# A decoder layer on one core: up-projection units 2 to 9 with the weights stationary, and one chain of the down-projection kept in PSUM over all groups

## The chip, the cores and the metric

The kernel runs on one core of a Trainium2 chip. The metric is the device time of one execution, in microseconds; three timed executions of the kernel before have a median of 1039.24 us (1039.18 to 1039.37). The profile is one more execution, recorded by the hardware profiler. Five engines work side by side and each takes its own instructions in order: PE (matrix products; PEld is its loading of the stationary operand), DVE and ACT (elementwise work, and the only two here that read PSUM), POOL and SP (here mostly queues that issue transfers).

## The reference, cut to what matters

The layer mixes a gated convolution, a pooling and an attention, adds the result to x, and then runs a feed-forward block. The change is in the feed-forward block alone:

```python
D_MODEL, SEQ = 2048, 256
D_FF = ((8 * D_MODEL // 3 + 255) // 256) * 256            # 5632
...
h = rmsnorm(x, g_ffn[l])
u = causal_dwconv(h @ w_up[l], ffn_conv_w[l]) + ffn_conv_b[l]   # 2 * D_FF columns, 3 taps over positions
gate, val = jnp.split(u, 2, axis=-1)
x = x + (jax.nn.silu(gate) * val) @ w_down[l]
return rmsnorm(x, g_final)
```

Everything is float32.

## The kernel before, in words

**Products.** A float32 product is made of three products of a narrower type. A weight tile that has landed in a `raw` buffer is split: ACT copies it to `hi` (rounded), DVE subtracts to get `lo`, the rest (`split_piece`, lines 131 and 132; for the down-projection's blocks `Blocks.split`, lines 254 and 255). The activations are held split as well. A product is high x hi, high x lo and low x hi. One tile of weights holds 128 x 2048 numbers, 1 MB. There are three `hi` buffers and three `lo` buffers, so that tile i can be split only when PE is done with tile i-3. Tiles are numbered in the order of `stream`; `next_tile` keeps loads three tiles and splits two tiles ahead of use.

**Units and groups.** The 5632 hidden columns are 11 units of 512. A unit has a gate part (w = 0) and a value part (w = 1), each 512 columns of `w_up`, and takes 8 tiles, called t0 to t7 below: four for the gate, four for the value. Units go in pairs as five groups (group 0 is units 0 and 1, and so on); unit 10 stands alone. Units 0 and 1 share a scheme of their own (`up_mixed`) that the change doesn't touch.

**`up` (lines 967 to 1006).** The activations are stationary (128 x 128) and the weights move, 512 columns at a time: a tile holds 4 blocks of 128 of the inner dimension, and is used by 2 blocks of tokens x 4 x 3 = 24 products of 512 columns. Results `pu` have tokens on the partitions, and after four tiles ACT scales them by each token's norm factor into `z` (line 1005). `up_finish` (lines 1071 to 1108) then turns `z` by 8 products with the identity (`pz`, line 1079) so that channels lie on the partitions, and works on each of the 4 blocks of channels: ACT applies the third tap and the bias (line 1087), DVE adds the other two taps (line 1089), ACT applies silu to gates (line 1093), and DVE multiplies value by gate into `u_raw`, a part of the buffer `ffn` (line 1103). The turning waits in the list `todo` and is run in the middle of the next tile.

**Down-projection.** When a group is done, `turn` builds eight combinations of its hidden values (`make_forms`, lines 881 to 899: seven DVE steps of 512 and one of 2048 elements, and ACT copies). While PE goes through the next group's units, `prod` is run 14 times between its tiles: seven products for each half of the output columns (p = 0 and 1), each of 12 matrix products on one tile of combined weights. The weights are combined by additions on DVE (`Blocks.add`, line 247) and by transfers that add (`Blocks.add_far`, line 244, on the POOL queue), issued from the splits of the products 0, 1 and 3. The seven products form three chains of sums in PSUM, `a`, `b` and `c`; a chain goes on adding in its bank, and after each product DVE adds the bank to the output rows `xt` (line 927). Chain `c` has one product, the sixth. The last group's p = 1 is done without combinations (`Plain`).

**Order.** `sched` gives the order by hand: no product in the first three tiles of a group, one after each of the next twelve, two after the last. So in the first unit of a group PE does t0, t1, t2, t3, product 0, t4, product 1, t5, product 2, t6, product 3, t7, product 4. The framework's scheduler then fixes the order of each engine's queue; it may pull single instructions of a later tile ahead where it takes them to be ready.

Of the kernel before, what the change touches and what calls it, by code (L numbers as in the profile page):

```python
# [9 lines left out]
F32 = mybir.dt.float32  # L10
F32R = mybir.dt.float32r
AF = mybir.ActivationFunctionType
# [3 lines left out]
P = 128  # L16
EPS = 1e-6
HPAD = 6
# [6 lines left out]
def kernel(  # L25
# [25 lines left out]
    def bank(name):  # L51
        return psum.tile([P, 512], F32, tag="bank", name=name)
# [42 lines left out]
    def cvec(name, i):  # L95
        c = col[name] + i
        return cols[:, c : c + 1]


    def src_a(w, k0, nk, c0, ncol):  # L100
        return w[k0 * P : (k0 + nk) * P, c0 : c0 + ncol].rearrange("(k p) c -> p k c", p=P)
# [52 lines left out]
    def next_tile():  # L154
        i = state["use"]
        state["use"] += 1
        advance(i + 1 + LOAD_AHEAD, i + 1 + SPLIT_AHEAD)
        return split.pop(i)
# [165 lines left out]
    def part_of(u, b):  # L324


        return (b // 2 % 2, b % 2 + b // 4 * 2) if u == 0 else (b // 4, b % 4)
# [50 lines left out]
                prods += [("plain" if isinstance(b, Plain) else "prod", b, i) for i in range(n)]  # L378
    for what, a, b in sched:
        if what == "up":  # L380
            w, q = part_of(a, b)
            plan_b(w_up, 4 * q, 4, w * D_UP + a * 512, 512, 4)
        elif what == "mixed" and isinstance(b, int):
            stream.append((up_blocks, None, b, 1))
        elif what == "mixed":
            plan_b(w_up, 4 * b[1], 4, (1 - b[0]) * D_UP + a * 512, 512, 4)
        else:
            stream.append((a, None, b, 1))
# [47 lines left out]
    def row_of(r, nm):  # L436

        pr = bank(f"prow_{nm}")
        row = cpool.tile([P, S], F32, name=f"row_{nm}")
        with tc.high_priority():  # L440
            for tb in range(TB):
                nc.tensor.transpose(
                    pr[:, tb * P : (tb + 1) * P], r[:, tb : tb + 1].to_broadcast([P, P]), ident
                )
            nc.scalar.activation(row, pr[:, :S], AF.Copy)
        return row
# [15 lines left out]
    def mm_a(ps, wt, actT, k0, nk, first, last):  # L462
        hi, lo = wt
        for kk in range(nk):
            k = k0 + kk
            cs = [slice(mi * P, (mi + 1) * P) for mi in range(len(ps))]
            for mi, c in enumerate(cs):
                nc.tensor.matmul(  # L468
                    ps[mi], hi[:, kk, c], actT[:, k, :], start=first and kk == 0, stop=False
                )  # L470
            for mi, c in enumerate(cs):
                nc.tensor.matmul(
                    ps[mi][:, S:], lo[:, kk, c], actT[:, k, :S],
                    start=False, stop=last and kk == nk - 1,
                )
# [123 lines left out]
    def split_into(o, src, n=S):  # L599

        nc.scalar.activation(o[:, :n], src, AF.Copy)
        nc.vector.tensor_tensor(o[:, n:], src, o[:, :n].bitcast(F32), op=ALU.subtract)
# [300 lines left out]
    def prod(bl, i):  # L903
        hi, lo = next_tile()

        chain, first, tb, right, op = (
            ("a", True, 0, 0, ALU.add),
            ("b", True, 1, 1, ALU.add),
            ("a", False, 0, 1, ALU.subtract),
            ("a", False, 1, 1, ALU.subtract),  # L910
            ("b", False, 0, 1, ALU.add),
            ("c", True, 0, 0, ALU.add),
            ("a", False, 1, 0, ALU.add),
        )[i]
        if first:
            chains[chain] = bank(f"pp_{bl.gi}_{bl.p}_{chain}")
        ps = chains[chain]
        for j in range(4):
            ah, al = bl.stationary(i, j)
            for n, (a, b) in enumerate(((ah, hi), (ah, lo), (al, hi))):  # L920
                nc.tensor.matmul(  # L921
                    ps, a, b[:, j, :], start=first and j == 0 and n == 0,
                    stop=j == 3 and n == 2, skip_group_check=True,
                )
        c0 = bl.p * 1024 + right * 512
        o = xt[:, tb, c0 : c0 + 512]
        nc.vector.tensor_tensor(o, o, ps, op=op)
# [34 lines left out]
    rawd = [ffn[:, 1 + i, :].rearrange("p (j c) -> p j c", c=512) for i in range(3)]  # L962

    u_last = h2T[:, : 4 * UNITS[-1], :]
    up_ps, up_gates, todo, r_2 = {}, {}, [], []

    def up(u, b):


        w, q = part_of(u, b)  # L970
        if q == 0:
            up_ps[w] = [bank(f"pu{u}_{w}_{tb}") for tb in range(TB)]
        ps = up_ps[w]
        hi, lo = next_tile()
        for tb in range(TB):
            for kk in range(4):
                k = 4 * q + kk
                ah = h2T[:, k, tb * P : (tb + 1) * P]
                al = h2T[:, k, S + tb * P : S + (tb + 1) * P]
                for n, (x_, y_) in enumerate(((ah, hi), (ah, lo), (al, hi))):  # L980
                    nc.tensor.matmul(  # L981
                        ps[tb], x_, y_[:, kk, :],
                        start=k == 0 and n == 0, stop=k == KC - 1 and n == 2,
                    )
            if tb == 0 and todo:
                todo.pop(0)()
        if u == 0 and b == 0:
            for k in range(8, 16, 2):
                split_turned(turn_pair(xt, k, "x2"), h2T, "g_ffn", k)
            r_2.append(rstd_sum(ssq4, "x2"))  # L990
        if u == 0 and b == 1:
            h2_8 = h2T[:, :8, :].bitcast(F32)
            nc.vector.tensor_tensor(u_raw, h2_8[:, :, :S], h2_8[:, :, S:], op=ALU.add)
            make_forms(
                u_raw, None, lambda half: sums[:, 1:5, half], (), "h2",
                up_blocks.buf("b12").rearrange("p j (f t) -> p j f t", t=P),
            )
            for name in ("b11", "b22", "b12"):
                up_blocks.load(name)
        if q < 3:  # L1000
            return
        z = []
        for tb in range(TB):
            z.append(spool.tile([P, 512], F32, tag="w2k", name=f"z_{u}_{w}_{tb}"))
            nc.scalar.activation(z[tb], ps[tb], AF.Copy, scale=r_2[0][:, tb : tb + 1])  # L1005
        todo.append(lambda: up_finish(u, w, z))

    def up_mixed(u, what):

# [61 lines left out]
    def up_finish(u, w, z):  # L1071

        pt = []
        for c in range(4):
            if c % 2 == 0:
                pt.append(bank(f"pz{u}_{w}_{c}"))
            for tb in range(TB):
                o = c % 2 * S + tb * P
                nc.tensor.transpose(pt[-1][:, o : o + P], z[tb][:, c * P : (c + 1) * P], ident)  # L1079
        outs = []  # L1080
        for c in range(4):
            v = pt[c // 2][:, c % 2 * S : (c % 2 + 1) * S]
            m = w * NF + u * 4 + c
            tag, n, bufs = ("w1k", S, 6) if w else ("hpad", PAD + S, HPAD)
            t = spool.tile([P, n], F32, tag=tag, name=f"t_{u}_{w}_{c}", bufs=bufs)[:, :S]
            cw = [cvec("ffn_conv_w", j * 2 * NF + m) for j in range(3)]
            nc.scalar.activation(t, v, AF.Identity, bias=cvec("ffn_conv_b", m), scale=cw[2])  # L1087
            for s in (1, 2):
                nc.vector.scalar_tensor_tensor(  # L1089
                    t[:, s:], v[:, : S - s], cw[2 - s], t[:, s:], op0=ALU.mult, op1=ALU.add  # L1090
                )
            if w == 0:
                nc.scalar.activation(t, t, AF.Silu)
            outs.append(t)
        if w == 0:
            up_gates[u] = outs
            return
        gates = up_gates.pop(u)
        gi = [g for g, (a, n) in enumerate(group_of) if a <= u][-1]
        for c in range(4):  # L1100
            if gi < len(group_of) - 1:
                o = u_raw[:, (u - group_of[gi][0]) * 4 + c, :]
                nc.vector.tensor_tensor(o, gates[c], outs[c], op=ALU.mult)
            else:
                nc.vector.tensor_tensor(gates[c], gates[c], outs[c], op=ALU.mult)
                split_into(u_last[:, c, :], gates[c])
        if gi < len(group_of) - 1 and u == group_of[gi][0] + group_of[gi][1] - 1:
            turn(gi)

    def turn(gi):  # L1110
        make_forms(
            u_raw, lambda at, half: sums[:, at, half], lambda half: sums[:, 1:5, half],
            (0, 5, 6, 7) if gi == len(group_of) - 2 else (0, 5, 6), gi,
        )
# [118 lines left out]
                finish(1, c0, c1, r)  # L1233

    for what, a, b in sched:
        {"up": up, "mixed": up_mixed, "prod": prod, "plain": plain}[what](a, b)
    down_last(len(group_of) - 1)


# [29 lines left out]
```

## Time and profile before

| | |
|---|---|
| time, median of 3 | 1039.24 us |
| the profiled execution, its own time | 1039.66 us |
| its span in the profile | 1037.9 us |
| PE busy | 1026.7 us, 99% of the span |
| DVE busy | 820.5 us, 79% |
| ACT busy | 601.8 us, 58% |
| moved between memory and chip | 224.97 MB, 217 GB/s |

The profile lists busy time per engine, then groups of equal instructions by line (count, busy time, mean duration, idle time ahead of them), and the chain of work that ended last, followed back from the end. Busy times of PE groups overlap each other, since its products are pipelined; what a product costs is read from the distance of starts in the timeline.

### The profile page before, as it was taken

The page shows a single profiled execution, that of the slowest core. Times are in us where ns is not written, and L with a number is a line of the kernel's source. Part 1 is how long each engine was busy: PE and PEld are TensorE (multiplying, and loading weights), DVE is VectorE, ACT ScalarE, POOL GpSimd, SP SyncE. Part 2 cuts the span into 40 slices and gives each one's busy share as a digit, 9 for nine tenths or more (in the row PEclk, how much of TensorE's full clock was granted, in tenths as well). Part 3 has the DMA queues.
Part 4 walks back from the last instruction along what each step waited for, and adds up shares of the span by engine and source line. Part 5 has one row for each costly group of instructions (what it writes and reads, how often), then busy time and mean ns, then how long its engine had stood idle before and what let it go on. Part 6 is the DMA issues. An engine that isn't in the chain of part 4 may idle for free.

```text
span 1037.9 us, 12624 instructions
## 1 busy us (share of the span) xinstructions
PE 1026.7 (99%) x4970; PEld 861.9 (83%) x4970; DVE 820.5 (79%) x866; ACT 601.8 (58%) x654; POOL 64.1 (6%) x97
## 2 busy tenths in 40 slices
PE   9999999999999999999999999999999999999996
PEld 7888888888888888888888888888888888888885
DVE  5677686777869688978779787797878978789776
ACT  5965454544556576655556556665566655665653
POOL 0023500000001000000000000000000000000000
PEclk9999999999999999999999999999999999999998
DMA  9765465557775687687966878668786697867832
GB/s 321 254 214 191 146 201 175 191 191 240 220 262 176 155 259 243 197 253 203 259 224 201 255 204 260 219 199 258 208 260 216 194 265 209 258 218 191 282 118 81
DMA packets 125157, 224.97 MB, mean 217 GB/s; under 512 B 3970, under 2 KB 36010, under 8 KB 124970
## 3 DMA queue, kind: packets, MB, share of 16 engines
q1 hardware_dynamic: 113450, 201.09, 57.2%
q0 software_dynamic: 11616, 23.07, 13.6%
q8 instruction: 39, 0.64, 0.2%
q14 instruction: 20, 0.16, 0.1%
q10 hardware_dynamic: 32, 0.01, 0.0%
HBM read 222.06 MB, written 2.10 MB: 216 GB/s over the span
## 4 chain that ended last, share of the span: by engine, by line
PE 98%; DMA 1%; DVE 0%; SPq 0%; DVEq 0%; issue 0%; ACT 0%
PE pu L981 42%; PE pp_a L921 9%; PE pp_b L921 5%; PE pp_c L921 2%; PE pa_cb L468 2%; PE pa_pv L468 2%; PE pa_cx L468 2%; PE pa_cc L468 2%; PE po L504 2%; PE pp L1127 2%; PE po L501 2%; PE po L507 2%; PE pz L1079 2%; PE pm_a L1024 2%; PE pa_q L468 1%; PE pk L558 1%
## 5 line engine op out<-in xcount | busy, mean ns | idle before, releaser
L981 PE MATMUL pu<-hi,h2T 128*128 128x512 f32 x1280 | 409.4, 391 | 0.0
L132 DVE TENSOR_TENSOR lo<-raw,hi 128x2048 fp32r<-128x2048 f32 (+3 forms) x148 | 314.7, 2128 | 70.9 <-ACT hi L131 69.9
L131 ACT ACTIVATE hi<-raw 128x2048 fp32r<-128x2048 f32 (+3 forms) x148 | 264.3, 1789 | 110.5 <-issue 34.7
L981 PEld LDWEIGHTS pu<-hi,h2T 128*128 128x128 f32 x1280 | 240.3, 188 | 49.4
L981 PE MATMUL pu<-lo,h2T 128*128 128x512 f32 x640 | 249.5, 390 | 0.0
L255 DVE TENSOR_TENSOR lo<-ffn,hi 128x2048 fp32r<-128x2048 f32 x70 | 160.3, 2290 | 72.0 <-ACT hi L254 72.0
L254 ACT ACTIVATE hi<-ffn 128x2048 fp32r<-128x2048 f32 x70 | 134.0, 1916 | 105.1 <-PE pu L981 75.0
L981 PEld LDWEIGHTS pu<-lo,h2T 128*128 128x128 f32 x640 | 120.2, 188 | 25.1 <-DVE lo L132 0.7
L921 PE MATMUL pp_a<-hi,sums 128*128 128x512 f32 x288 | 94.5, 389 | 0.0
L1089 DVE SCALAR_TENSOR_TENSOR t<-pz,cols,t 128x255 f32<-128x255 f32 (+1 forms) x176 | 79.6, 478 | 10.2 <-ACT t L1087 9.2
L1087 ACT ACTIVATE t<-pz,cols 128x256 f32<-128x256 f32 x88 | 46.9, 558 | 48.1 <-DVE t L1089 24.2
L921 PEld LDWEIGHTS pp_a<-hi,sums 128*128 128x128 f32 x288 | 54.1, 188 | 11.2
L244 POOL DMA_DIRECT2D ffn<-in_w_down_dram x18 | 23.1, 1284 | 575.8 <-DVE ffn L247 454.3
L921 PE MATMUL pp_a<-lo,sums 128*128 128x512 f32 x144 | 56.0, 389 | 0.0
L1005 ACT ACTIVATE z<-pu,r_x 128x512 f32<-128x512 f32 x40 | 27.4, 686 | 39.7 <-PE pu L981 39.6
L247 DVE TENSOR_TENSOR ffn<-ffn 128x2048 f32<-128x2048 f32 x20 | 45.7, 2287 | 3.4 <-DMA ffn<-in_w_up_dram 3.4
L921 PE MATMUL pp_b<-hi,sums 128*128 128x512 f32 x144 | 47.3, 389 | 0.0
L921 PEld LDWEIGHTS pp_a<-lo,sums 128*128 128x128 f32 x144 | 27.0, 188 | 5.6
L921 PEld LDWEIGHTS pp_b<-hi,sums 128*128 128x128 f32 x144 | 27.0, 188 | 5.6
L468 PE MATMUL pa_cb<-hT,hi 128*128 128x512 f32 x96 | 30.7, 400 | 0.0
L468 PE MATMUL pa_pv<-hT,hi 128*128 128x512 f32 x96 | 30.2, 396 | 0.0
L468 PE MATMUL pa_cc<-hT,hi 128*128 128x512 f32 x96 | 30.2, 395 | 0.0
(292 smaller groups left out, 1477.1 us busy)
## 6 DMA issues: line engine op xcount, KB each, us to landing
raw<-in_w_up_dram SPq DMA_DIRECT2D x84, 1024.0 KB, 7.5
ffn<-in_w_down_dram SPq DMA_DIRECT2D x40, 1024.0 KB, 6.1
raw<-in_w_in_dram SPq DMA_DIRECT2D x28, 1024.0 KB, 5.0
ffn<-in_w_down_dram POOLq DMA_DIRECT2D x18, 1024.0 KB, 10.3
raw<-in_w_out_dram SPq DMA_DIRECT2D x12, 1024.0 KB, 5.1
raw<-in_w_kv_dram SPq DMA_DIRECT2D x4, 1024.0 KB, 7.3
outp<-in_w_out_dram SPq DMA_DIRECT2D x4, 1024.0 KB, 7.5
ffn<-in_w_up_dram SPq DMA_DIRECT2D x4, 1024.0 KB, 5.5
```

The lines of the kernel that those rows point to most:

```text
L131: nc.scalar.activation(hi[:, s, :], raw[:, s, :], AF.Copy)
L132: nc.vector.tensor_tensor(lo[:, s, :], raw[:, s, :], hi[:, s, :].bitcast(F32), op=ALU.subtract)
L244: nc.gpsimd.dma_start(self.buf(to), self.source(what), accum_op=ALU.add)
L247: nc.vector.tensor_tensor(self.buf(to), self.buf(to), self.buf(what), op=ALU.add)
L254: nc.scalar.activation(hi, raw, AF.Copy)
L255: nc.vector.tensor_tensor(lo, raw, hi.bitcast(F32), op=ALU.subtract)
L468: nc.tensor.matmul(ps[mi], hi[:, kk, c], actT[:, k, :], start=first and kk == 0, stop=False)
L921: nc.tensor.matmul(ps, a, b[:, j, :], start=first and j == 0 and n == 0, stop=j == 3 and n == 2, skip_group_check=True,)
L981: nc.tensor.matmul(ps[tb], x_, y_[:, kk, :], start=k == 0 and n == 0, stop=k == KC - 1 and n == 2,)
L1005: nc.scalar.activation(z[tb], ps[tb], AF.Copy, scale=r_2[0][:, tb : tb + 1])
L1087: nc.scalar.activation(t, v, AF.Identity, bias=cvec("ffn_conv_b", m), scale=cw[2])
L1089: nc.vector.scalar_tensor_tensor(t[:, s:], v[:, : S - s], cw[2 - s], t[:, s:], op0=ALU.mult, op1=ALU.add)
```

## The change

Units 2 to 9 go through a new function `up_turned`. A tile now holds 8 blocks of the inner dimension and 256 columns, and the weights are stationary: `mm_a`, which the input projection already uses, takes for each of the 8 blocks and each of the 2 sets of 128 columns one product of 512 moving columns (both parts of the activations with `hi`) and one of 256 (`lo`). Results have channels on the partitions at once, so that the turning by the identity and `z` are gone; a pair of 128-channel blocks is finished after two tiles, so that a unit has four pairs instead of two parts of four blocks. The norm factor, which was a scale per partition, becomes a row (`row_of`, once) that DVE multiplies by. Chain `c` of each half of the output keeps its bank over all groups and is added to `xt` once, after the last group that uses combinations.

```diff
     for what, a, b in sched:
         if what == "up":
+            if 1 < a < n_units - 1:
+                stream.append(
+                    (src_a(w_up, b % 2 * 8, 8, b // 4 * D_UP + a * 512 + b // 2 % 2 * 256, 256), 8, 256, 1)
+                )
+                continue
...
+        done = True
+        if chain == "c" and bl.gi is not None:
+
+            chain = f"c{bl.p}"
+            first = chain not in chains
+            done = not any(type(b) is Blocks and b.p == bl.p and b.gi > bl.gi for b in blocks)
...
+        if not done:
+            return
         c0 = bl.p * 1024 + right * 512
...
+    def up_turned(u, b):
...
+        w, pair, h = b // 4, b // 2 % 2, b % 2
+        if h == 0:
+            up_ps[w] = [bank(f"pu{u}_{w}_{pair}_{mi}") for mi in range(2)]
+        hi, lo = next_tile()
+        for e in range(2):
+            kk = slice(4 * e, 4 * e + 4)
+            mm_a(
+                up_ps[w], (hi[:, kk, :], lo[:, kk, :]), h2T, h * 8 + 4 * e, 4,
+                h == 0 and e == 0, h == 1 and e == 1,
+            )
+            if e == 0 and todo:
+                todo.pop(0)()
+        if h == 0:
+            return
+        if not row_2:
+            row_2.append(row_of(r_2[0], "x2"))
+        v = spool.tile([P, 2, S], F32, tag="w2k", name=f"v_{u}_{w}_{pair}")
+        for mi, p_ in enumerate(up_ps[w]):
+            nc.scalar.activation(v[:, mi, :], p_[:, S:], AF.Copy)
+            nc.vector.tensor_tensor(v[:, mi, :], p_[:, :S], v[:, mi, :], op=ALU.add)
+        row = row_2[0].rearrange("p (o t) -> p o t", o=1).to_broadcast([P, 2, S])
+        nc.vector.tensor_tensor(v, v, row, op=ALU.mult)
...
+            nc.scalar.activation(
+                t, v[:, mi, :], AF.Identity, bias=cvec("ffn_conv_b", m), scale=cw[2]
+            )
+            for s in (1, 2):
+                nc.vector.scalar_tensor_tensor(
+                    t[:, s:], v[:, mi, : S - s], cw[2 - s], t[:, s:], op0=ALU.mult, op1=ALU.add
+                )
+            if w == 0:
+                nc.scalar.activation(t, t, AF.Silu)
...
+                nc.vector.tensor_tensor(o, g, t, op=ALU.mult)
+        if w and pair:
...
+            elif u == a + n - 1:
+                todo.append(lambda: turn(gi))
...
     for what, a, b in sched:
-        {"up": up, "mixed": up_mixed, "prod": prod, "plain": plain}[what](a, b)
+        f = up_turned if what == "up" and 1 < a < n_units - 1 else None
+        (f or {"up": up, "mixed": up_mixed, "prod": prod, "plain": plain}[what])(a, b)
```

What the change does to the queues is shown at two places. Both are in unit 4, the first unit of group 2. Its tiles t4, t5 and t6 are numbers 110, 112 and 114 of the stream, and the products 0, 1 and 2 between them are 109, 111 and 113; `hi_112` and `lo_112` are the two halves of tile 112.

First, the queue of DVE up to the split of t5 (tile 112). Before:

```order
L895 TENSOR_TENSOR turn_1_4449<-turn_1_4449,ffn_2844 128x512
L247 TENSOR_TENSOR ffn_2844<-ffn_2844 128x2048
L899 TENSOR_TENSOR sums_2843<-turn_1_4449,sums_2843 128x4x512
L132 TENSOR_TENSOR lo_110_4535<-raw_110_4502,hi_110_4534 128x2048
L927 TENSOR_TENSOR xt_90<-xt_90,pp_1_0_a_4573 128x512
L255 TENSOR_TENSOR lo_111_4569<-ffn_2844,hi_111_4568 128x2048
L132 TENSOR_TENSOR lo_112_4590<-raw_112_4566,hi_112_4589 128x2048
L247 TENSOR_TENSOR ffn_2844<-ffn_2844 128x2048
```

And now, from the split of t4 to that of t5 (lines of the changed kernel: 1043 adds the two halves of a result, 1045 multiplies by the row, 1058 is a tap, 940 the addition to `xt`; `v_4_0_1` is the gate's second pair, which t3 completes):

```order
L132 TENSOR_TENSOR lo_110_4708<-raw_110_4667,hi_110_4707 128x2048
L1043 TENSOR_TENSOR v_4_0_1_4743<-pu4_0_1_0_4665,v_4_0_1_4743 128x256
L1043 TENSOR_TENSOR v_4_0_1_4743<-pu4_0_1_1_4666,v_4_0_1_4743 128x256
L255 TENSOR_TENSOR lo_111_4762<-ffn_2844,hi_111_4761 128x2048
L1045 TENSOR_TENSOR v_4_0_1_4743<-v_4_0_1_4743,row_x2_3622 128x512
L247 TENSOR_TENSOR ffn_2844<-ffn_2844 128x2048
L1058 SCALAR_TENSOR_TENSOR t_4_0_2_4749<-v_4_0_1_4743,cols_86,t_4_0_2_4749 128x255
L1058 SCALAR_TENSOR_TENSOR t_4_0_3_4754<-v_4_0_1_4743,cols_86,t_4_0_3_4754 128x255
L1058 SCALAR_TENSOR_TENSOR t_4_0_2_4749<-v_4_0_1_4743,cols_86,t_4_0_2_4749 128x254
L1058 SCALAR_TENSOR_TENSOR t_4_0_3_4754<-v_4_0_1_4743,cols_86,t_4_0_3_4754 128x254
L940 TENSOR_TENSOR xt_90<-xt_90,pp_1_0_a_4766 128x512
L132 TENSOR_TENSOR lo_112_4783<-raw_112_4759,hi_112_4782 128x2048
```

Between the splits of t4 and t5 there stood one addition to `xt` and one split (`lo_111`); now the finish of a pair (seven steps) stands there too, and the second weight addition of line 247, which came after `lo_112`.

Second, the queue of PE at the start of t5. Before:

```order
L921 MATMUL pp_1_0_b_4653<-hi_111_4568,sums_2843 128x512 x2
L921 MATMUL pp_1_0_b_4653<-lo_111_4569,sums_2843 128x512
L921 MATMUL pp_1_0_b_4653<-hi_111_4568,sums_2843 128x512
L981 MATMUL pu4_1_0_4587<-hi_112_4589,h2T_2275 128x512
L981 MATMUL pu4_1_0_4587<-lo_112_4590,h2T_2275 128x512
L981 MATMUL pu4_1_0_4587<-hi_112_4589,h2T_2275 128x512 x2
```

And now:

```order
L932 MATMUL pp_1_0_b_4824<-hi_111_4761,sums_2843 128x512 x2
L932 MATMUL pp_1_0_b_4824<-lo_111_4762,sums_2843 128x512
L932 MATMUL pp_1_0_b_4824<-hi_111_4761,sums_2843 128x512
L473 MATMUL pu4_1_0_0_4780<-h2T_2275,hi_112_4782 128x512
L473 MATMUL pu4_1_0_1_4781<-h2T_2275,hi_112_4782 128x512
L932 MATMUL pp_1_0_a_4766<-hi_113_4820,sums_2843 128x512
L473 MATMUL pu4_1_1_0_4911<-h2T_2275,hi_114_4838 128x512
L477 MATMUL pu4_1_0_0_4780<-h2T_2275,lo_112_4783 128x256
L477 MATMUL pu4_1_0_1_4781<-h2T_2275,lo_112_4783 128x256
```

One product of tile 113 and one of tile 114 now stand ahead of the first one that needs `lo_112`. The other groups' first units (units 2, 6 and 8) read the same at this place.

## Rows read from the trace of the kernel before

**Rows 1.** The page's first part (busy time, share of the span and instructions of each engine) and its fourth (the chain that ended last, by engine).

```profile
PE 1026.7 (99%) x4970; PEld 861.9 (83%) x4970; DVE 820.5 (79%) x866; ACT 601.8 (58%) x654; POOL 64.1 (6%) x97
...
PE 98%; DMA 1%; DVE 0%; SPq 0%; DVEq 0%; issue 0%; ACT 0%
```

**Rows 2.** Windows: the input projection's stretch, then group 2 (units 4 and 5) whole and cut in two, the first part being its first unit. Columns: start:end, length, busy us (instructions) of PE, PEld, DVE, ACT and POOL, the granted clock, the busy share of the 16 DMA engines, GB/s.

```profile
60.00:215.00 155.00, 155.00 (x921) 135.95 (x920) 111.80 (x170) 76.73 (x106) 27.77 (x49) 1.00 0.58 188
530.00:659.00 129.00, 129.00 (x586) 106.84 (x585) 106.91 (x97) 76.03 (x66) 5.13 (x4) 1.00 0.78 228
530.00:590.00 60.00, 60.00 (x273) 49.58 (x272) 53.65 (x50) 35.91 (x34) 2.56 (x2) 1.00 0.73 217
590.00:659.00 69.00, 69.00 (x314) 57.26 (x313) 53.26 (x47) 40.12 (x33) 2.56 (x2) 1.00 0.82 238
```

**Rows 3.** Timeline of PE around the start of unit 4 and at its t4 and t5: start, length, line, output<-inputs, shapes, count.

```profile
529.88 0.39 PE L921 MATMUL pp_a<-hi,sums 128*128 128x512 f32 x1
...
532.60 0.39 PE L981 MATMUL pu<-hi,h2T 128*128 128x512 f32 x1
...
535.33 1.04 PE L1079 MATMUL pz<-ident,z 128*128 128x128 f32 x8
...
555.26 0.39 PE L921 MATMUL pp_a<-hi,sums 128*128 128x512 f32 x1
...
557.98 0.40 PE L981 MATMUL pu<-hi,h2T 128*128 128x512 f32 x1
...
564.62 0.39 PE L921 MATMUL pp_b<-hi,sums 128*128 128x512 f32 x1
...
567.34 0.39 PE L981 MATMUL pu<-hi,h2T 128*128 128x512 f32 x1
567.56 0.39 PE L981 MATMUL pu<-lo,h2T 128*128 128x512 f32 x1
```

**Rows 4.** Timeline of PE in the input projection, which uses `mm_a`: the first two rows are one block, and the last is the start of the block 22 later.

```profile
59.63 0.63 PE L468 MATMUL pa_q<-hT,hi 128*128 128x512 f32 x2
60.10 0.39 PE L472 MATMUL pa_q<-hT,lo 128*128 128x256 f32 x2
...
74.96 0.63 PE L468 MATMUL pa_q<-hT,hi 128*128 128x512 f32 x2
```

**Rows 5.** Groups of instructions of DVE by line and shape, over the whole span: count | busy us, mean ns of one | idle us ahead of them and what ended it.

```profile
L132 DVE TENSOR_TENSOR lo<-raw,hi 128x2048 fp32r<-128x2048 f32 x127 | 290.5, 2288 | 63.6 <-ACT hi L131 63.2
...
L247 DVE TENSOR_TENSOR ffn<-ffn 128x2048 f32<-128x2048 f32 x20 | 45.7, 2287 | 3.4 <-DMA ffn<-in_w_up_dram 3.4
L1089 DVE SCALAR_TENSOR_TENSOR t<-pz,cols,t 128x255 f32<-128x255 f32 x88 | 41.3, 480 | 9.2 <-ACT t L1087 9.2
...
L1103 DVE TENSOR_TENSOR ffn<-t,t 128x256 f32<-128x256 f32 x40 | 16.0, 421 | 0.4
...
L927 DVE TENSOR_TENSOR xt<-xt,pp_c 128x512 f32<-128x512 f32 x9 | 6.1, 678 | 0.0
L843 DVE SCALAR_TENSOR_TENSOR cv<-cu,cols,cv 128x256 f32<-128x256 f32 x12 | 5.3, 480 | 0.0
...
L486 DVE TENSOR_TENSOR cc<-pa_cc,cc 128x256 f32<-128x256 f32 x6 | 2.4, 412 | 0.0
```

**Rows 6.** The same view for ACT: the copies to `hi`, the copy of one half of a result in the input projection, and the scaling of the up-projection's results.

```profile
L131 ACT ACTIVATE hi<-raw 128x2048 fp32r<-128x2048 f32 x127 | 243.5, 1918 | 110.1 <-issue 34.7 <-PE po L507 14.6 <-PE pp_a L921 13.1
...
L1005 ACT ACTIVATE z<-pu,r_x 128x512 f32<-128x512 f32 x40 | 27.4, 686 | 39.7 <-PE pu L981 39.6
...
L485 ACT ACTIVATE cc<-pa_cc 128x256 f32<-128x256 f32 x6 | 2.1, 374 | 0.0
```

**Rows 7.** Timeline of DVE in unit 4: start, length, line, operation, count, idle time ahead. The split of `ffn` is tile 111, the split of `raw` behind it tile 112.

```profile
556.25 2.29 DVE L132 TENSOR_TENSOR lo<-raw,hi 128x2048 fp32r<-128x2048 f32 x1
558.46 0.68 DVE L927 TENSOR_TENSOR xt<-xt,pp_a 128x512 f32<-128x512 f32 x1
559.06 2.28 DVE L255 TENSOR_TENSOR lo<-ffn,hi 128x2048 fp32r<-128x2048 f32 x1
561.26 2.29 DVE L132 TENSOR_TENSOR lo<-raw,hi 128x2048 fp32r<-128x2048 f32 x1
563.47 2.28 DVE L247 TENSOR_TENSOR ffn<-ffn 128x2048 f32<-128x2048 f32 x1
...
570.34 1.65 DVE L1089 SCALAR_TENSOR_TENSOR t<-pz,cols,t 128x255 f32<-128x255 f32 x4
```

**Rows 8.** Timeline of DVE in unit 2, the first of group 1, around the split of its t5 (tile 82, the first row).

```profile
434.26 2.29 DVE L132 TENSOR_TENSOR lo<-raw,hi 128x2048 fp32r<-128x2048 f32 x1
436.46 1.00 DVE L1089 SCALAR_TENSOR_TENSOR t<-pz,cols,t 128x255 f32<-128x255 f32 x2
```

**Rows 9.** Timeline of PE at the same place: the start of t5 with its first product of `lo_82`.

```profile
438.32 0.39 PE L981 MATMUL pu<-hi,h2T 128*128 128x512 f32 x1
438.54 0.39 PE L981 MATMUL pu<-lo,h2T 128*128 128x512 f32 x1
```

**Rows 10.** The page's sixth part: transfers by line, count, KB each, median us from issue to landing.

```profile
raw<-in_w_up_dram SPq DMA_DIRECT2D x84, 1024.0 KB, 7.5
...
raw<-in_w_in_dram SPq DMA_DIRECT2D x28, 1024.0 KB, 5.0
...
ffn<-in_w_down_dram POOLq DMA_DIRECT2D x18, 1024.0 KB, 10.3
```

More of the change, by code (lines that the diff above doesn't have):

```diff
@@ L964 @@
     u_last = h2T[:, : 4 * UNITS[-1], :]
-    up_ps, up_gates, todo, r_2 = {}, {}, [], []
+    up_ps, up_gates, todo, r_2, row_2 = {}, {}, [], [], []
     def up(u, b):
@@ L1006, in up @@
         todo.append(lambda: up_finish(u, w, z))
+    def up_turned(u, b):
[21 more added lines that the diff above has]
+        nc.vector.tensor_tensor(v, v, row, op=ALU.mult)
+        gi = [g for g, (a, n) in enumerate(group_of) if a <= u][-1]
+        a, n = group_of[gi]
+        for mi in range(2):
+            c = pair * 2 + mi
+            m = w * NF + u * 4 + c
+            tag, n_c, bufs = ("w1k", S, 6) if w else ("hpad", PAD + S, HPAD)
+            t = spool.tile([P, n_c], F32, tag=tag, name=f"t_{u}_{w}_{c}", bufs=bufs)[:, :S]
+            cw = [cvec("ffn_conv_w", j * 2 * NF + m) for j in range(3)]
+            nc.scalar.activation(
[7 more added lines that the diff above has]
+                nc.scalar.activation(t, t, AF.Silu)
+                up_gates[u, c] = t
+            else:
+                g = up_gates[u, c]
+                last = gi == len(group_of) - 1
+                o = g if last else u_raw[:, (u - a) * 4 + c, :]
+                nc.vector.tensor_tensor(o, g, t, op=ALU.mult)
+        if w and pair:
+            if gi == len(group_of) - 1:
+                for c in range(4):
+                    split_into(u_last[:, c, :], up_gates[u, c])
+            elif u == a + n - 1:
+                todo.append(lambda: turn(gi))
```

## The prediction

> **What bounds the kernel now.** I read the busy shares first: PE is busy 99% of the span, and the chain that ended last is PE for 98% of it [rows 1]. [...] So a change in the up-projection is worth what it does to PE's queue: products that become dearer or go, and new stops of PE for another engine. The engine to watch is DVE: in the first unit of group 2 it is busy 53.65 of 60 us, in the rest of the group 53.26 of 69 us [rows 2]. The sum is made against the profiled execution, 1039.66 us with a span of 1037.9 us, and then set off from the median of 1039.24 us, 0.42 us lower.
>
> **The tiles get dearer.** Twelve products of 512 columns take 532.60 - 529.88 = 2.72 us [rows 3], 0.2267 us each, so a tile of 24 takes 5.44 us. The new tile is eight blocks of `mm_a`, each of two products of 512 and two of 256 columns. The input projection has the same blocks, with the same width of weights: 22 of them take 74.96 - 59.63 = 15.33 us [rows 4], 0.697 us each, so a tile takes 5.57 us. That is 0.136 us more (with the division carried on), and 8 units of 8 tiles make **+8.7 us**. The columns fed are the same; a product of 256 costs 0.122 us here, more than half of one of 512, (0.697 - 2 x 0.2267) / 2.
>
> [...]
>
> **The transposes go.** The four tiles at the start of unit 4 with eight transposes among them take 555.26 - 532.60 = 22.66 us, where 96 products are 21.76 us [rows 3]: 0.90 us for eight. Units 2 to 9 lose sixteen times eight: **-14.4 us**. At t4 they cost more: 557.98 to 564.62 is 6.64 us [rows 3], 1.20 us over 5.44 us. 0.3 us more in groups 2 to 4 (the ones where I saw it): **-0.9 us**. Turning the norm factor into a row, once, adds some small products: +0.2 us, by the price of two transposes.
>
> **What DVE gets.** Per 128-channel block the four taps of a pair, the gating and the silu stay. New are, per pair, two additions of 256 elements (412 ns in the input projection) and one multiplication of 512 (as 678 ns) [rows 5]; the scaling of `z` on ACT (686 ns for each two blocks' worth) is replaced by two copies (374 ns) [rows 6]. Back to back, a step ends some 0.08 us before the next one's start plus its length (559.06 to 561.26 is 2.20 us for one of 2.28) [rows 7], so a pair's finish is 2 x 0.34 + 0.60 + 4 x 0.40 = 2.88 us, of which 1.28 us is new; a unit's four pairs add 5.1 us. Seven of the nine additions of `pp_c` go, 0.60 us each [rows 5]. A first unit comes to (53.65 + 5.1) / 60 = 98% of DVE, the rest of a group to (53.26 + 5.1) / 69 = 85%. The first unit of a group is where four products' additions and splits lie, and there DVE also gets its work earlier: before, the gate's finish came all at once in the middle of t4, behind the split of t5 (`lo_112`); now the pairs of t1 and t3 are queued ahead of it (the order shows that of t3).
>
> **The new wait at t5 of units 2, 4, 6 and 8.** *Group 1*: the split `lo_82` ends at 434.26 + 2.29 = 436.55 [rows 8] and is wanted at 438.54 [rows 9], 2.0 us to spare. Two pairs ahead of it are 5.76 us, and I add 0.4 us for steps that wait for their ACT copy: 442.7. Wanted: five tiles dearer (+0.68), the transposes of t4 gone (-0.92), the row (+0.2), and one more product of `hi` ahead (+0.23): 438.7. So 4.0 us late, of which 0.45 us is filled by the two products that the queue now has there from tiles 83 and 84: 3.5 us. *Groups 2 to 4*: `lo_112` ends at 561.26 + 2.29 = 563.55 [rows 7], wanted at 567.56 [rows 3], 4.0 us to spare. DVE's list gets +5.76 (two pairs), -1.0 (the old unit's last pair is 3.56 in place of 4.56 us), -0.60 (a `pp_c`), +2.21 (the weight addition of line 247, moved ahead): +6.4, and it starts some 0.8 us earlier, since transposes are gone from t0: 569.2. Wanted: 567.56 - 1.20 - 0.90 + 0.68 + 0.23 = 566.4. Late 2.8, less 0.45: 2.4 us at most.
>
> From below, PE's queue has one product of `hi_114` ahead of `lo_112`. With three buffers `hi_114` needs that of tile 111, free when product 1 ends, and the copy takes ACT 1.92 us [rows 6]. PE has three products to do meanwhile (0.68 us): a stop of about 1.3 us however early DVE is. I take 2.0 us for each of groups 2 to 4, nearer to the upper end since two bounds act at once. Together 3.5 + 3 x 2.0 = **+9.5 us**; the ends are 3.0 + 3 x 1.3 = 6.9 and 4.0 + 3 x 3.0 = 13.
>
> Queued behind the late split on DVE are line 247's and the next products' splits, so t6 starts late too; PE stood still as long, so I count no second stop. In units 3, 5, 7 and 9 no products' weights are combined at t1 to t6 to that degree, and my walk leaves 0.5 us at the tightest split; nothing, but 2 to 4 us in all if that cover is gone.
>
> **At nothing.** Transfers: rows of 1 KB in place of 2 KB. The input projection loads such rows at 188 GB/s with a share of 0.58, group 2 has 228 GB/s at 0.78 [rows 2]; per byte that is 0.0031 against 0.0034, so no sign that the queues fill. A tile landed 5.0 us after issue there, 7.5 us now [rows 10], and is issued three tiles (16 us) ahead; the transfers that add take 10.3 us [rows 10], and all transfers together end 1% of the chain [rows 1]. PSUM: two banks for `c0`, `c1`, two for `a`, `b` and two pairs of two are eight; a pair's banks are wanted again 11 us after they are full, and its additions are done within about 5 us.
>
> **Sum.** 8.7 + 0.2 - 14.4 - 0.9 + 9.5 = +3.1 us: 1042.8 us against the profiled execution, 1042.3 us against the median. The ends of the wait alone give +0.5 and +6.6 us.
>
> **Rivals.**
> *The waits are the floor alone.* If `lo` of t5 is ready within 1.3 us of its time, since the scheduler's order on DVE is kinder than my walk or steps overlap more, four stops of 1.3 us give 5.2: net -1.2, 1038.0 us. For it: 2 us of spare before. Against: 5.76 us ahead in the queue.
> *No stop.* The copies and splits are as early as before: 8.7 + 0.2 - 14.4 - 0.9 = -6.4, so 1032.8 us. Against it are both bounds above; for it, PE ran 24 products a tile without a stop at 89% of DVE.
> *DVE is full.* If steps from different tiles don't overlap by 0.08 us (each waits for its ACT copy: 23 steps a group by 0.08, 4 groups, 7.4 us), or the second units lose their 0.5 us: 1045 to 1049 us. It decides from a DVE share over 98% in the first unit. This is the far end of slower, and the forecast's own sum is the near one.
> [...]
> [...]
>
> **Chances.** The forecast (1040.3 to 1046) 0.48; floor 0.27; no stop 0.10; DVE full 0.10; taps 0.03; cheap 256 0.02. A measurement of this kernel tells 0.2%, about 2.1 us, from no change. Faster: no stop 0.10, cheap 256 0.02, 0.04 of the floor: 0.16. Same (1037.2 to 1041.3): 0.23 of the floor, 0.03 of the taps, 0.07 of the forecast: 0.33. Slower: 0.41 of the forecast and 0.10: 0.51. The range must leave out the no-stop end and the far end of a full DVE: 1035.5 to 1047.0 us; the forecast alone is 1040.3 to 1046.
>
> **What would show it.** Blocks in units 2 to 9 every 0.697 us and no `pz` there, or the first two terms are wrong. PE idle at t5 of units 2, 4, 6 and 8 for 1.3 to 3.5 us, released by `lo` of line 132 (or by `hi` of line 131: then the floor); no stop there speaks for the second rival, stops in the second units for the third. DVE busy up by 8 x 5.1 - 4 = 37 us, and some 98% in the first units. A stop released by a transfer or by a bank would be something that I have left out.

## The result, and the profile after

The changed kernel takes 1042.43 us (1042.23 to 1042.72, 8 runs) against 1039.23 us, a ratio of 1.0031 with a 95% interval of 1.0022 to 1.0040: slower by 3.2 us, where 3.1 us was forecast. The forecast of 1042.3 us was met within 0.2 us partly by luck: errors in the sum offset each other.

First the page: busy time by engine and the chain that ended last, then the transfers of `w_up`.

```profile
PE 1023.0 (98%) x5356; PEld 873.1 (84%) x5356; DVE 851.2 (82%) x955; ACT 602.6 (58%) x687; POOL 64.2 (6%) x97
...
PE 84%; DVE 11%; issue 3%; ACT 1%; DVEq 0%; ACTq 0%
...
raw<-in_w_up_dram SPq DMA_DIRECT2D x84, 1024.0 KB, 6.4
```

Against [rows 1] PE is busy 3.7 us less, and the chain is 84% PE instead of 98%: DVE is on it now, busy 30.7 us more (I had expected 37). Transfers land sooner than in [rows 10], 6.4 instead of 7.5 us, and no product of units 2 to 9 waits for one; rows of 1 KB cost nothing here. Next, what PE waited for, over the whole span (total, times, longest), and the windows of group 2 cut at its first unit, to be set beside [rows 2].

```profile
PE pu L473 <- ACT hi L131: 6.0, 4, 1.7
PE pp_a L932 <- ACT t L1062: 1.2, 1, 1.2
```

```profile
534.00:594.00 60.00, 58.56 (x318) 50.17 (x317) 56.83 (x61) 35.42 (x36) 2.56 (x2) 1.00 0.75 212
594.00:663.00 69.00, 69.00 (x366) 59.10 (x364) 57.70 (x58) 40.93 (x39) 2.56 (x2) 1.00 0.84 243
```

Four stops of PE for `hi`, and a fifth in group 1. In the first unit DVE rises from 53.65 to 56.83 of 60 us, 95% and not the 98% that I gave; in the rest of the group PE is busy throughout. The place is t5 of unit 4. First PE, then DVE and ACT there (line 132 is `lo_112`, the ACT copy `hi_114`):

```profile
569.82 0.39 PE L932 MATMUL pp_b<-hi,sums 128*128 128x512 f32 x1
570.05 0.62 PE L473 MATMUL pu<-h2T,hi 128*128 128x512 f32 x2
570.50 0.39 PE L932 MATMUL pp_a<-hi,sums 128*128 128x512 f32 x1
572.33 0.50 PE L473 MATMUL pu<-h2T,hi 128*128 128x512 f32 x1 [1.44 <-ACT hi L131]
572.66 0.40 PE L477 MATMUL pu<-h2T,lo 128*128 128x256 f32 x2
```

```profile
569.94 2.28 DVE L132 TENSOR_TENSOR lo<-raw,hi 128x2048 fp32r<-128x2048 f32 x1
```

```profile
569.76 0.71 ACT L1062 ACTIVATE t<-t 128x256 f32<-128x256 f32 x2
570.38 1.90 ACT L131 ACTIVATE hi<-raw 128x2048 fp32r<-128x2048 f32 x1
```

`hi_114` is done at 572.28 and `lo_112` at 572.22: the two bounds of the prediction meet within 0.06 us, and the view of waits can name but one of them. The stop in group 1 is of another kind. PE, then ACT there, then windows of 3 and 1 us behind it (the column ahead of the last two is the granted clock):

```profile
437.99 0.61 PE L473 MATMUL pu<-h2T,hi 128*128 128x512 f32 x2
439.76 0.47 PE L932 MATMUL pp_a<-hi,sums 128*128 128x512 f32 x1 [1.16 <-ACT t L1062]
441.91 0.79 PE L473 MATMUL pu<-h2T,hi 128*128 128x512 f32 x1 [1.68 <-ACT hi L131]
442.50 0.63 PE L477 MATMUL pu<-h2T,lo 128*128 128x256 f32 x2
442.93 1.05 PE L473 MATMUL pu<-h2T,hi 128*128 128x512 f32 x2
443.78 0.63 PE L477 MATMUL pu<-h2T,lo 128*128 128x256 f32 x2
```

```profile
437.54 1.91 ACT L254 ACTIVATE hi<-ffn 128x2048 fp32r<-128x2048 f32 x1 [1.16 <-DVE ffn L247]
```

```profile
442.00:445.00 3.00, 3.00 (x9) 2.58 (x10) 3.00 (x3) 0.00 (x0) 0.68 (x1) 0.50 0.69 204
445.00:446.00 1.00, 1.00 (x7) 0.83 (x6) 1.00 (x1) 0.00 (x0) 0.60 (x1) 0.97 1.09 374
```

Two stops (1.32 and 1.92 us by the starts). The first is one that the prediction didn't have: the product of tile 83 needs `hi_83`, which ACT copies only after the weight addition of line 247, itself late behind the finish of pairs on DVE, is done at 437.45 (the view names the silu that follows the copy on ACT). It adds nothing to the total, since `lo_82`, done at 441.82, holds PE longer; e4 below has one stop of 3.21 us here. Then two products of 512 take 443.78 - 442.93 = 0.85 us where they took 0.45 before the stop: the granted clock is at 0.50. By the starts up to 445.3 us that costs another 1.5 us.

### The profile page after: what moved, and what is told of

It is laid out like the page before. It is cut to its first block, busy times and chain, and to the rows that moved or that the text cites. A ratio compares the mean times of both kernels' runs of the same rounds, so it can differ in the third digit from the quotient of the medians.

```text
span 1040.7 us, 13534 instructions
## 1 busy us (share of the span) xinstructions
PE 1023.0 (98%) x5356; PEld 873.1 (84%) x5356; DVE 851.2 (82%) x955; ACT 602.6 (58%) x687; POOL 64.2 (6%) x97
## 4 chain that ended last, share of the span: by engine, by line
PE 84%; DVE 11%; issue 3%; ACT 1%; DVEq 0%; ACTq 0%
PE pu L473 16%; PE pu L994 8%; PE pu L477 8%; PE pp_a L932 8%; PE pp_b L932 4%; DVE lo L132 3%; PE pa_cb L473 2%; PE pa_cx L473 2%; PE pa_cc L473 2%; PE pa_pv L473 2%; PE po L506 2%; PE pp L1195 2%; PE po L512 2%; PE po L509 2%; PE pp_c L932 2%
## 5 line engine op out<-in xcount | busy, mean ns | idle before, releaser
L473 PE MATMUL pu<-h2T,hi 128*128 128x512 f32 x1024 | 323.3, 396 | 6.0 <-ACT hi L131 6.0
L477 PEld LDWEIGHTS pu<-h2T,lo 128*128 128x128 f32 x1024 | 193.0, 189 | 45.3 <-DVE lo L132 0.3
L477 PE MATMUL pu<-h2T,lo 128*128 128x256 f32 x1024 | 201.8, 278 | 0.0
L473 PEld LDWEIGHTS pu<-h2T,hi 128*128 128x128 f32 x1024 | 160.3, 189 | 11.4 <-ACT hi L131 7.5
L994 PE MATMUL pu<-hi,h2T 128*128 128x512 f32 x256 | 81.0, 390 | 0.0
L1054 ACT ACTIVATE t<-v,cols 128x256 f32<-128x256 f32 x64 | 35.0, 594 | 43.7 <-DVE v L1045 43.7
L994 PEld LDWEIGHTS pu<-hi,h2T 128*128 128x128 f32 x256 | 48.1, 188 | 9.8
L1058 DVE SCALAR_TENSOR_TENSOR t<-v,cols,t 128x254 f32<-128x254 f32 (+1 forms) x128 | 53.1, 475 | 0.0
L994 PE MATMUL pu<-lo,h2T 128*128 128x512 f32 x128 | 49.8, 389 | 0.0
L473 PE MATMUL pa_cb<-hT,hi 128*128 128x512 f32 x96 | 30.7, 400 | 0.0
```

The lines of the kernel that those rows point to most:

```text
L473: nc.tensor.matmul(ps[mi], hi[:, kk, c], actT[:, k, :], start=first and kk == 0, stop=False)
L477: nc.tensor.matmul(ps[mi][:, S:], lo[:, kk, c], actT[:, k, :S], start=False, stop=last and kk == nk - 1,)
L994: nc.tensor.matmul(ps[tb], x_, y_[:, kk, :], start=k == 0 and n == 0, stop=k == KC - 1 and n == 2,)
L1054: nc.scalar.activation(t, v[:, mi, :], AF.Identity, bias=cvec("ffn_conv_b", m), scale=cw[2])
L1058: nc.vector.scalar_tensor_tensor(t[:, s:], v[:, mi, : S - s], cw[2 - s], t[:, s:], op0=ALU.mult, op1=ALU.add)
```

## The experiments

My theory, after this: a stop at t5 ends with the later of two things, `lo` of t5, which stands behind the finish of pairs on DVE, and `hi` of a later tile whose product PE's queue has ahead of it. The rivals: the buffer alone sets the stop; or DVE is simply full, so that a stop taken away here comes back elsewhere.

**One part alone.** e1 has the turned units without the kept chain:

```diff
-        if chain == "c" and bl.gi is not None:
+        if False:
```

> Up-projection units 2 to 9 turned as in the changed kernel, chain c as before (added to xt after every sixth product). Theory (a stop at t5 ends with the later of lo of t5, which stands behind DVE's list, and the product of a later tile that PE's queue has ahead): here the scheduler puts four taps of the last pair (1.6 us) behind the split of t5 in groups 2 to 4 and one more addition of pp_c (0.6 us) ahead, and PE's queue has no product of t6 ahead there; the stop of 1.6 us in each of these groups falls to 0.7 us, group 1 keeps its own: 1039.5 us, 1038.5 to 1041. Rival (the stop is that of the buffer, or of DVE's total work): 1042.5 us or more, since seven additions come back.

1040.61 us, ratio 1.0012 (1.0004 to 1.0021), inside the range and 1.1 us over the figure. PE and DVE at t5 of unit 4:

```profile
570.76 0.39 PE L932 MATMUL pp_a<-hi,sums 128*128 128x512 f32 x1
571.93 0.51 PE L477 MATMUL pu<-h2T,lo 128*128 128x256 f32 x2 [0.78 <-DVE lo L132]
```

```profile
569.59 2.28 DVE L132 TENSOR_TENSOR lo<-raw,hi 128x2048 fp32r<-128x2048 f32 x1
571.79 1.65 DVE L1058 SCALAR_TENSOR_TENSOR t<-v,cols,t 128x255 f32<-128x255 f32 x4
```

The four taps stand behind the split now, and the stop is 571.93 - 570.76 - 0.23 = 0.94 us, where 0.7 us was expected, released by `lo`. With more to do for DVE the kernel is 1.8 us faster than with the chain kept: what counts is DVE's list ahead of this split, not its total.

e2 has the kept chain without the turned units (`up` for all):

```diff
-            if 1 < a < n_units - 1:
+            if False:
...
-        f = up_turned if what == "up" and 1 < a < n_units - 1 else None
+        f = None
```

> Units 2 to 9 as in the kernel before, chain c kept in PSUM over all groups. Theory: seven additions of 0.6 us leave DVE, which nobody on the chain waits for: 1039.2 us, within 0.4. Rival: the two banks that are held narrow PSUM and a product waits for one: 1040 or more; or the additions were on the path: 1035.

1038.52 us, ratio 0.9992 (0.9983 to 1.0001): a gain of 0.8 us, just short of being told from none, and outside my 0.4 us. The trace shows a gain at t4. The eight transposes stand together there,

```profile
560.23 1.03 PE L1147 MATMUL pz<-ident,z 128*128 128x128 f32 x8
```

where before they were cut in two, and a group takes 128.72 us from t0 to t0 instead of 129.07 (in [rows 3] t0 starts at 532.60). So the 0.3 us per group that I gave to the transposes of t4 goes with the chain alone, by the order of the queue. The two parts alone are worth +1.3 and -0.8 us; together +3.2.

**The order on DVE.** e3 is the changed kernel with the finish of a pair put off to the middle of the unit's next tile, as `up` has it:

```diff
+        ps = up_ps[w]
+        todo.append(lambda: turned_finish(u, w, pair, ps))
+
+    def turned_finish(u, w, pair, ps):
...
-                todo.append(lambda: turn(gi))
+                turn(gi)
```

> The changed kernel, with the finish of a pair put off to the middle of the next tile of the unit, so that on DVE the split of t5 stands ahead of the pair of t3 (2.9 us). Theory: lo of t5 comes 2.9 us earlier, PE's queue no longer has products of t6 ahead of it in groups 2 to 4, and the four stops go but for 0.5 us in group 1: 10.2 us less, 1032.5 us (1031.8 to 1033.5), granted clock at full in group 1. Rival (DVE is full in the first units): the stops move to t6 or t7 or into the second units, 1038 to 1042.

1033.43 us, ratio 0.9944 (0.9930 to 0.9957): faster than both kernels, 9.0 us below the changed one. The starts of t0 of groups 2 and 3, then the split and the wanted product at t5 of unit 4 (the profiled run is 1.6 us over the median, all of it ahead of the feed-forward block, so lengths are used, not times):

```profile
534.06 0.62 PE L473 MATMUL pu<-h2T,hi 128*128 128x512 f32 x2
...
567.82 0.40 PE L477 MATMUL pu<-h2T,lo 128*128 128x256 f32 x2
...
661.32 0.61 PE L473 MATMUL pu<-h2T,hi 128*128 128x512 f32 x2
```

```profile
565.31 2.29 DVE L132 TENSOR_TENSOR lo<-raw,hi 128x2048 fp32r<-128x2048 f32 x1
```

`lo_112` is done at 567.60, 0.22 us ahead of its product. That is 33.54 us after t0, 1.9 us sooner than the 35.48 us of the changed kernel, not the 2.9 us that I expected; part of the difference is that DVE now waits 0.67 us for ACT in t0 (the row stands below, with e8). A group takes 127.26 us; the changed kernel takes 128.98 from t0 to t0:

```profile
536.74 0.62 PE L473 MATMUL pu<-h2T,hi 128*128 128x512 f32 x2
...
665.72 0.62 PE L473 MATMUL pu<-h2T,hi 128*128 128x512 f32 x2
```

So a stop there cost 1.7 us. In group 1 0.54 us of stop is left, and the clock stays at 1.00. The stops are gone and come back nowhere, while DVE is as full as before (57.44 of the 60 us from 531, 56.83 in the changed kernel's first unit): the rival falls, though 0.22 us is a thin cover.

**How thin.** e8 is e3 with chain `c` as before (the edit of e1):

> The kernel of e3 with chain c as in the kernel before. Theory: the seven additions come back to a DVE that PE no longer waits for: 1033.4 us, within 0.6. Rival (the chain's part is worth what it took off DVE, or the order shifts again): 1034.5 us or more.

1037.32 us, ratio 0.9983 (0.9973 to 0.9992). My expectation was wrong, and its rival right. At t5 of unit 4 PE stops twice:

```profile
566.81 0.50 PE L932 MATMUL pp_a<-hi,sums 128*128 128x512 f32 x1 [0.26 <-ACT hi L254]
567.60 0.50 PE L477 MATMUL pu<-h2T,lo 128*128 128x256 f32 x2 [0.29 <-DVE lo L132]
```

The addition of 0.6 us alone doesn't give this. DVE in t0 of unit 4, first e3, then e8:

```profile
539.86 1.40 DVE L1063 SCALAR_TENSOR_TENSOR t<-v,cols,t 128x255 f32<-128x255 f32 x3 [0.67 <-ACT t L1059]
```

```profile
539.93 2.29 DVE L132 TENSOR_TENSOR lo<-raw,hi 128x2048 fp32r<-128x2048 f32 x1 [1.68 <-ACT hi L131]
```

With the addition there, the scheduler puts a split ahead of the taps, and DVE stands 1.68 us for its `hi` where it stood 0.67 us. So `lo_112` comes 35.09 us after t0 instead of 33.54: 0.6 us by the addition and 1.0 us by the order. On PE a product of tile 113 stands ahead of it again, and that one waits first, for its `hi`. A group is 1.3 us longer than in e3. The kept chain, worth nothing measurable by itself, is worth 3.9 us on top of e3, more by the order that it changes than by the time of its additions.

**The order on PE.** e4 leaves DVE's queue as in the changed kernel, row for row, and keeps products of later tiles out of t5:

```diff
+    def after_last():
+        return tc.issue_after(ends[-1]) if ends else nullcontext()
...
-            mm_a(
-                up_ps[w], (hi[:, kk, :], lo[:, kk, :]), h2T, h * 8 + 4 * e, 4,
-                h == 0 and e == 0, h == 1 and e == 1,
-            )
+            with after_last():
+                ends.append(mm_a(
+                    up_ps[w], (hi[:, kk, :], lo[:, kk, :]), h2T, h * 8 + 4 * e, 4,
+                    h == 0 and e == 0, h == 1 and e == 1,
+                ))
```

(and the same around the products of `prod`).

> The changed kernel, with the products of each tile in units 2 to 9 queued behind the last product of the turned tile ahead of them, so that no product of hi of t6 stands ahead of lo of t5; DVE's queue is the same row for row. Theory: lo of t5 is as late by itself (572.2 against hi_114 at 572.3 in unit 4), so the stops stay at 1.6 to 1.8 us in groups 2 to 4 and 3.4 us in group 1: 1042.4 us (1041 to 1043, the lower end if the clock does not fall in group 1). Rival (the buffer of t6 sets the stop): the stops of groups 2 to 4 go, 1037.5 us.

1043.70 us, ratio 1.0046 (1.0033 to 1.0059), 0.7 us above my range. PE in units 2 and 4, and the clock behind the stop of unit 2:

```profile
438.46 0.61 PE L474 MATMUL pu<-h2T,hi 128*128 128x512 f32 x2
442.12 0.79 PE L478 MATMUL pu<-h2T,lo 128*128 128x256 f32 x2 [3.04 <-DVE lo L133]
...
571.99 0.61 PE L474 MATMUL pu<-h2T,hi 128*128 128x512 f32 x2
574.07 0.50 PE L478 MATMUL pu<-h2T,lo 128*128 128x256 f32 x2 [1.47 <-DVE lo L133]
```

```profile
442.00:448.00 6.00, 5.88 (x19) 5.11 (x20) 5.07 (x4) 0.10 (x1) 1.28 (x1) 0.50 0.75 200
448.00:449.00 1.00, 1.00 (x7) 0.81 (x6) 0.00 (x0) 0.00 (x0) 0.00 (x0) 0.88 1.05 176
```

Without `hi_114` the stops of groups 2 to 4 are 574.07 - 571.99 - 0.45 = 1.63 us, as long as before: `lo` alone holds them, and the rival that the buffer sets them falls. The traced run, 1044.79 us, is 2.3 us above that of the changed kernel. 1.6 us of this is lost in group 1, where the clock stays at 0.50 for twice as long, and 0.18 us in each of groups 2 to 4. The median is 1.1 us lower than the traced run, so how long the clock was down in the other runs isn't known. Whether the buffer alone would give a stop of its own was not tried; in e3, where DVE's list is shorter, PE's queue has no product of `hi_114` ahead of `lo_112`.

**The two large terms by themselves.** e5 is e3 with each product of 512 columns in units 2 to 9 made as two of 256:

```diff
+                for x_ in (slice(0, S), slice(S, 2 * S)) if cut else (slice(0, 2 * S),):
...
+                        ps[mi][:, x_], hi[:, kk, c], actT[:, k, x_],
```

> The kernel of e3, with each product of 512 columns in units 2 to 9 made as two of 256: 16 more products in each of 64 tiles, the columns fed unchanged. Theory (a product costs its columns and a fixed 14 ns: 227 ns for 512, 120 ns for 256): 1024 products by 14 ns, 14.3 us more than e3, 1047.7 us (1046 to 1050). Rival (the dearer tile comes from the change of the stationary operand's kind, not from the number of products): no more than 3 us over e3, 1036 us.

1045.77 us, 12.3 us over e3 and a little under my range: 12.0 ns for each of 1024 products, where 14 was my estimate. The columns fed are the same, so the 12.0 ns are what a further product, with the loading of its stationary operand (one for each product on the page above), cost here beside its columns. A tile of 32 products in place of 24 is dearer by 8 x 12.0 = 96 ns for this, 6.1 us over 64 tiles; the tiles measured 8.3 us (below), and the other 2 us are not explained.

e6 is the kernel before without the turning in units 2 to 9; the finish reads `z`, so its hidden values are not turned:

```diff
-        pt = []
-        for c in range(4):
+        pt = z if 1 < u < n_units - 1 else []
+        for c in range(4) if not pt else ():
```

> The kernel before, with the turning by the identity left out in units 2 to 9 (the finish reads z where it read pz, so hidden values are not turned). Theory: the term as I had it, sixteen times eight transposes at 0.90 us and 0.3 us more at three places, 15.3 us less: 1024.0 us (1023.3 to 1024.8), with no stop, as the finish is as far behind the split of t5 as before. Rival: the transposes are partly covered by time that PE would wait anyway, 1028 us or more.

1023.63 us, ratio 0.9851 (0.9837 to 0.9865): 15.6 us less, against 15.3 expected.

**Trying for more.** e7 is e3 with unit 10 turned too:

```diff
-            if 1 < a < n_units - 1:
+            if 1 < a:
...
-        f = up_turned if what == "up" and 1 < a < n_units - 1 else None
+        f = up_turned if what == "up" and 1 < a else None
```

> The kernel of e3 with unit 10 turned as well. Theory: eight tiles at 0.13 us more (+1.0), sixteen transposes less (-1.8), 0.8 us less by PE's queue, and the last finish comes a pair at a time, so that the last products wait no longer than before: 1032.6 us (1031.8 to 1033.4). Rival: the last pair's finish, put off into the products of the last group, comes later than the whole finish did and PE waits for it: 1034 to 1036.

1034.24 us, ratio 0.9957 (0.9944 to 0.9970), 0.8 us over e3, the wrong way (the intervals overlap, but the lower runs lie at 1034.2 us, those of e3 at 1033.4 to 1033.6). Its stops in unit 10, at t4 and t5:

```profile
940.62 0.51 PE L477 MATMUL pu<-h2T,lo 128*128 128x256 f32 x2 [0.52 <-DVE lo L132]
949.22 0.50 PE L932 MATMUL pp_a<-hi,sums 128*128 128x512 f32 x1 [0.24 <-ACT hi L254]
950.00 0.50 PE L477 MATMUL pu<-h2T,lo 128*128 128x256 f32 x2 [0.29 <-DVE lo L132]
```

By the starts they are 1.6 us together. Neither theory had them: not the end but the middle of the unit lost time, to the same list on DVE. So e9 and e10 take work off that list: e3 and e7 with the multiplication by the row on POOL.

```diff
-        nc.vector.tensor_tensor(v, v, row, op=ALU.mult)
+        nc.gpsimd.tensor_tensor(v, v, row, op=ALU.mult)
```

> The kernel of e3 with the multiplication by the row on POOL, which is idle there. Theory (DVE's list ahead of the split decides): 0.6 us less ahead of the split of t5 per pair, so that the stop of 0.54 us in group 1 and the 0.35 us at unit 10 go: 1032.6 us (1032.0 to 1033.2). Rival (the slower multiplication, 1.2 us for 256 elements and so about 2.4 us for 512, stands ahead of the taps in DVE's queue, which wait for it): DVE stops and PE behind it, 1035 us or more.

> The kernel of e7 with the multiplication by the row on POOL. Theory: the stops of unit 10 (1.6 us in e7) and of group 1 go, and the 0.8 us of e7's products show: 1032.0 us (1031.3 to 1032.8). Rival, as for e9: 1035 us or more.

1050.61 us, ratio 1.0107 (1.0092 to 1.0122), and 1053.14 us, ratio 1.0132 (1.0115 to 1.0148): the rival, and far beyond its bound. POOL, ACT and DVE of e9 at one pair of unit 4:

```profile
559.04 5.10 POOL L1050 TENSOR_TENSOR v<-v,row_x 128x512 f32<-128x512 f32 x1
```

```profile
564.18 1.10 ACT L1059 ACTIVATE t<-v,cols 128x256 f32<-128x256 f32 x2 [4.22 <-POOL v L1050]
```

```profile
560.71 2.28 DVE L255 TENSOR_TENSOR lo<-ffn,hi 128x2048 fp32r<-128x2048 f32 x1
564.81 1.77 DVE L1063 SCALAR_TENSOR_TENSOR t<-v,cols,t 128x255 f32<-128x255 f32 x4 [1.82 <-ACT t L1059]
```

The multiplication takes 5.10 us, ACT's third tap waits for it, DVE's taps wait for ACT, and all splits behind them in DVE's queue come later. By the starts PE stops 2.38 us at t5 of this unit, and a group takes 131.9 us where e3 takes 127.26. Work was taken off a queue and a wait put into it.

## Why the prediction was right

By its own terms, predicted and measured:

| term | predicted | measured | from |
|---|---|---|---|
| 64 dearer tiles | +8.7 | +8.3 | a tile and a product take 8.29 us after, 5.44 + 2.72 = 8.16 before |
| transposes | -15.3 | -15.6 | e6 |
| the row | +0.2 | +0.2 | group 1's first four tiles: 0.72 us longer, 0.52 of it the tiles |
| stop in group 1 | +3.5 | +4.8 | 3.24 us of stop and 1.53 us of clock |
| stops in groups 2 to 4 | +6.0 | +5.2 | 128.98 against 127.26 us in e3, three times |
| sum | +3.1 | +2.9 | spans 1037.9 and 1040.7 us: +2.8; medians +3.2 |

The 8.29 us are two starts of t-tiles in group 1 with one product between, at the full clock:

```profile
467.67 0.61 PE L473 MATMUL pu<-h2T,hi 128*128 128x512 f32 x2
...
475.96 0.62 PE L473 MATMUL pu<-h2T,hi 128*128 128x512 f32 x2
```

*What bounds the kernel*: right, inside the stages too [rows 2]; PE's queue priced the two large terms within 5%, and DVE was the engine to watch. *The tiles*: right in size; e5 gives most of the cause that the prediction left open, a price per product (6.1 of 8.3 us). *The transposes*: right, but the 0.3 us at t4 belonged to the order of PE's queue, which the chain alone also mends (e2).

*Groups 2 to 4*: the mechanism was right, the size 0.3 us too large each. I had `lo_112` 36.6 us after t0 and its product wanted at 33.8; it came 572.22 - 536.74 = 35.5 us after, and the product was free to go at 33.8. A pair took 2.85 us where I counted 2.88, so that was not it: before, DVE stood 0.75 us, most of it for ACT, between its split at 532.69 and `lo_112`, and after, not at all between the same two splits; and of the old unit's last pair the additions were done ahead of them. Both made the list shorter than my walk; the floor, which I set at 1.3 us, was 1.6, as ACT had a silu to end before `hi_114`. That both bounds act was right, and e4 shows that `lo` suffices; whether the buffer does is open.

*Group 1*: the lateness of 3.5 us was right (3.24 us), but the step "3.5 us late costs 3.5 us" left out what PE does after the stop: the clock went to half for 3 us. The 1.3 us missing here is what the 0.8 us too much in the other groups, 0.4 in the tiles and 0.3 too little for the transposes made up for. That the total came out is luck to this extent; the terms are each within 1.3 us.

*Chain c*: this was the weak step. I gave it 0.60 us in the list ahead of `lo_112` and no other effect. The additions were off the path before, and e2 moves little; but with the turned units DVE's list ahead of t5 has no slack, and the chain also changes the order that the scheduler chooses, so that it is worth 3.9 us in one kernel (e8 against e3) and costs 1.8 us in another (the changed kernel against e1). *Rivals*: the floor alone falls by e4 and by the 3.24 us of group 1, no stop at all by the trace, a full DVE by the windows (95% in the first unit, and PE busy 69.00 of 69 us in the second). Two of the chances are for things that no run shows, faster taps (0.03) and a cheap product of 256 columns (0.02): the taps took 475 ns on average where line 1089 took 478, and a product of 256 comes to (226.7 + 12.0) / 2 = 119 ns by e5, more than half of the 226.7 ns of one of 512, while the tiles cost 8.3 us more.

## What to carry to other kernels

A change that takes work off the bounding engine is worth that work minus the stops that it makes, and these hang on what stands ahead of one late instruction in the in-order queue of the helper engine, not on that engine's busy share. Here the same work in another order (e3) turned +3.2 us into -5.8 us. Before moving work to an idle engine, look who waits for it in which queue: an order costs nothing to change, a slower step in the middle of a chain does (0.69 us on DVE in e3, up to 5.10 us on POOL in e9, and 17.2 us more for the kernel).

## What the runs showed of the hardware

After a stop of 3.2 us, whole (e4) or with one product in it (the changed kernel), the granted clock was 0.50 for over 6 us and 3 us; after stops of 1.6 us it stayed at 1.00. After a stop of 2.4 us it did one or the other. In e9 and e10 PE stops 2.36 to 2.39 us by the starts at t5 of each of groups 2 to 4, and the clock fell behind four of these six stops. Two of e9, each followed by a window of the 3 us behind it:

```profile
571.64 0.73 PE L477 MATMUL pu<-h2T,lo 128*128 128x256 f32 x2 [2.22 <-DVE lo L132]
...
835.52 0.50 PE L477 MATMUL pu<-h2T,lo 128*128 128x256 f32 x2 [2.22 <-DVE lo L132]
```

```profile
572.00:575.00 3.00, 3.00 (x11) 2.61 (x11) 2.44 (x2) 0.59 (x1) 2.61 (x1) 0.50 0.80 251
836.00:839.00 3.00, 3.00 (x19) 2.61 (x18) 2.33 (x2) 0.48 (x1) 2.72 (x1) 1.00 0.80 261
```

So the length of the stop alone doesn't decide, and what does is open. The eleven runs of e1 lie at 1039.0 to 1039.1, 1040.5 to 1040.8 and 1042.3 to 1042.9 us, with a mean granted clock of 0.997, 0.995 to 0.996 and 0.994 to 0.995; the traced one, of the middle group, had 0.50 for about 3 us in group 1. This fits none, one and two such stretches, but only that run was traced. A step of about 1.6 us is no proof by itself: the kernel before, which has no such stop, has runs at 1040.8 to 1041.1 as well as at 1038.9 to 1039.6, and in e3's traced run the 1.6 us were lost near the start, where four products of 512 took 1.84 us (6.79 to 8.63) and in e7 0.99.

The 128x512 multiplication on POOL took 2.13 us on average (68.2 us for 32) in e9, and the average hides three cases: 1.29 us where no split ran on DVE (at 455.31), 3.26 us where one did (at 535.02) and 5.10 us where two did (at 559.04). Over 1.29 us that is 1.97 and 3.81 us, and the splits still ran 2.10 and 3.95 us when it began: it gained next to nothing while they ran. Why it did so the trace doesn't show.
